# A decoder layer on one Trainium2 core: the down projection's splits and sums put in program order, twelve norm multiplications spread over six halves, and sums made ahead begun and ended sooner

## The chip, the cores and the metric

One core of a Trainium2 chip runs the whole layer in one launch. The engines named below are TensorE (PE; PEld is its weight load), VectorE (DVE), ScalarE (ACT), GpSimdE (POOL) and SyncE (SP). Each works through its own instructions in the order in which they are queued and waits on semaphores for the others; DMAs are issued from the queues of SP, ACT and POOL. The metric is device time in microseconds (us), and lower is better. The kernel before takes 1496.49 us (median of 3 runs, 1496.36 to 1498.1).

## The reference, cut to what matters

```python
BATCH, SEQ, D_MODEL, D_FF = 1, 256, 2048, 8192          # float32 throughout
def reference(x, ...):
    h = rmsnorm(x, norm_mix_pre)
    proj = h @ w_in                                      # 2048 x 13312
    xr, yr, q, k, v, g_rnn, g_attn = split(proj)
    y_rnn = rg_lru(causal_conv(xr)) * gelu(yr)
    y_att = sliding_window_sink_attention(rope(q), rope(k), v, sinks)
    mix = sigmoid(g_rnn) * (y_rnn @ w_rnn_proj) + sigmoid(g_attn) * (y_att @ w_attn_proj)
    x = x + rmsnorm(mix @ w_out, norm_mix_post)
    h = rmsnorm(x, norm_mlp_pre)
    u = square(relu(h @ w_mlp_up))                       # 256 x 8192
    x = x + rmsnorm(u @ w_mlp_down, norm_mlp_post)       # the down projection: 8192 x 2048
    return x
def rmsnorm(x, g):
    return x * rsqrt(mean(x * x, -1) + 1e-6) * g
```

## The kernel before, in words

**Tiling.** The 256 rows of x stand as two blocks of 128 (`TB = 2`). Every float32 matrix product is made of three TensorE products of two-part operands: high times high, high times low, low times high, each 128 x 128 by 128 x 512 (or 256) columns, accumulated in a PSUM bank. So each piece of weight has to be split. The class `Stream` does that for all weights in one fixed order: a weight chunk of 128 x 2048 is two halves of 128 x 1024, numbered through the whole kernel. For half j, SP loads `wraw j` (every fifth half `xraw` in the later stages), ACT copies it, rounded, to `whi j` (line 104), and DVE subtracts the two to get `wlo j` (line 105). There are 4 rooms for raw halves (`WRAW`), 6 for high parts and 6 for low parts (`WHALF`). A raw room comes free when its low part has been made, and only then SP's next load can go; a high or low room comes free when TensorE has used its content.

**The stages.** The input projections, attention, the recurrent branch and the gates take the first half of the time. Then the output projection, here the o pass (matmuls on lines 327 to 331, halves 240 to 271); then the MLP, cut into two parts f = 0 and f = 1 of 4096 columns of u each: up f = 0, down f = 0 (two column halves of the output, n = 0 from about 981 us and n = 1 from about 1063 us), up f = 1, down f = 1 (n = 0 from about 1322 us, n = 1 from about 1403 us).

**The down projection.** The 16 pairs of chunks of one (f, n) come as halves 336 to 367 (f = 0, n = 0), 368 to 399, 464 to 495 and 496 to 527. Ten of the 16 pairs (nine for f = 1) are done with seven products instead of eight (`seven`): their right operands are four quarters of the raw pair and three sums of quarters. `right_sums` (lines 59, 61 and 62) makes the three sums `t`, `t` and `t4` on DVE, `two_parts` splits the two raw halves into `whi`/`wlo`, and the inner function `split` makes `thi` (ACT, line 148) and `tlo` (DVE, line 149) of the three sums. For some of those pairs the three sums were made long before by the generator `sums_ahead` (POOL loads four quarters, DVE adds them, POOL writes the sums and the changed half away to DRAM), and come back by DMA as `second`. TensorE's products of the down projection are all on line 1178. Their banks are P1, P6, Q5, N7 (tiles `s0`, `s1`), and `dP2`, `dQ3`, `dQ4`, `dCs`.

After the last seven-product pair, `down` merges the four banks of `s0` and `s1`: an ACT copy of P1 (line 1227) and DVE sums on lines 1228 to 1231 (in f = 1 also line 1324, `early`). The last two pairs of each (f, n) are "held": their four halves stay in their rooms and are used for one output bank after the other, so that each bank is finished while TensorE works on the next. `finish` adds the merged sum to the bank: for f = 0 on line 1312, with a DMA on ACT's queue to `acc_away` behind it (line 1313); for f = 1, n = 0 on lines 1347 and 1348; for f = 1, n = 1 on lines 1352 to 1372, which end the kernel.

**What sets the order.** A scheduler places the instructions of each engine by estimated times when the kernel is built, within the dependencies. `tc.keep_in_program_order` pins an instruction behind the one traced before it on its engine; `tc.issue_after(i)` puts what a block traces behind instruction i on i's engine. In the kernel before, the splits and sums of the down projection are not pinned; a `ws.pin` that does nothing is set before the MLP.

**The norm's weight multiplications.** Before the o pass, twelve DVE multiplications of 128 x 512 are traced as a block: four of `gp` by `g2` (line 949) and eight of `x1` by `g2` (line 954).

**Sums made ahead.** `sums_ahead(c, gaps, rooms)` is run a step at a time by `ws.begin`, once per half or pair; `gaps` are the steps it waits between its loads, its sums and its writes. Six are put in the list ahead of the gates, with gaps (1, 3, 1); four are put there in up f = 0 at pair 2 (`R2_AT`), with gaps (1, 5, 1).

## Time and profile before

| | before |
|---|---|
| median of 3 runs | 1496.49 us |
| profiled execution, its own time | 1495.03 us |
| its span, first to last instruction | 1493.3 us |
| mean granted TensorE clock | 0.999 |
| PE busy | 1479.2 us (99%) |
| DVE busy | 1139.9 us (76%) |
| ACT busy | 852.7 us (57%) |
| POOL busy | 77.5 us (5%) |
| DMA, mean over the span | 229 GB/s |

The profile is one execution; the outside of its span is 1495.03 - 1493.3 = 1.7 us. A row of the timeline gives start, duration, engine, line, operation, out<-in, shapes and count, and in brackets the idle time of the engine just before with what ended it. Matmuls overlap: one 128 x 512 product starts 0.23 us after the one ahead of it though its record is 0.39 us long, so a stall of TensorE is read from starts.

### The profile page before, as it was taken

The numbers are of one execution on the slowest core, as the hardware profiler recorded it, in microseconds if no ns is written. First come the engines' busy times: TensorE is split into PE (matmuls) and PEld (weight loads), VectorE is DVE, ScalarE is ACT, GpSimd is POOL, SyncE is SP. The second block draws the span as 40 slices with busy tenths as digits, with TensorE's granted clock in tenths as the row PEclk, the third lists the DMA queues.
The fourth block names the chain that finished last, engine by engine and source line by source line (L and its number), as shares of the span: only waits on it lengthen the run. The fifth ranks groups of instructions, "written<-read, shape, count | busy, mean of one in ns | idle before, by whom it ended". The sixth has DMA issues, their size and how long they took to land.

```text
span 1493.3 us, 20560 instructions
## 1 busy us (share of the span) xinstructions
PE 1479.2 (99%) x7556; PEld 1252.9 (84%) x7556; DVE 1139.9 (76%) x1503; ACT 852.7 (57%) x1236; POOL 77.5 (5%) x149
## 2 busy tenths in 40 slices
PE   9999999999999999999999999999999999999997
PEld 7887778888888888888789888888878888888886
DVE  7676668749668866666667877799987777789897
ACT  8564565647467675444355665556564545556563
POOL 0000000000000001110000011010110111000000
PEclk9999999999999999999999999999999999999999
DMA  9754544555646667886775877678778777678584
GB/s 341 228 167 141 177 165 135 176 189 178 203 157 207 201 205 253 309 291 238 288 237 171 286 266 266 215 252 279 242 268 297 251 258 249 200 279 275 190 275 165
DMA packets 96901, 342.38 MB, mean 229 GB/s; under 512 B 11552, under 2 KB 11808, under 8 KB 95776
## 3 DMA queue, kind: packets, MB, share of 16 engines
q1 hardware_dynamic: 80352, 288.89, 57.2%
q0 software_dynamic: 12992, 44.05, 8.4%
q10 hardware_dynamic: 3456, 8.13, 1.5%
q8 instruction: 59, 0.97, 0.3%
q14 instruction: 42, 0.34, 0.1%
HBM read 316.38 MB, written 24.64 MB: 228 GB/s over the span
## 4 chain that ended last, share of the span: by engine, by line
PE 83%; DVE 9%; DMA 5%; issue 2%; ACT 1%; DVEq 0%; SPq 0%; ACTq 0%
PE ps L289 21%; PE ps L287 11%; PE g L327 4%; PE g L331 4%; PE g L329 4%; PE pp L329 4%; PE pp L327 4%; PE pp L331 4%; PE dQ L1178 4%; DVE wlo L105 3%; PE s L1178 3%; DMA wraw<-in_w_dn 3%; PE q L327 2%; PE dP L1178 2%; PE q L331 2%; PE q L329 2%
## 5 line engine op out<-in xcount | busy, mean ns | idle before, releaser
L105 DVE TENSOR_TENSOR wlo<-wraw,whi 128x1024 fp32r<-128x1024 f32 x469 | 567.7, 1221 | 240.1 <-ACT whi L104 236.3
L104 ACT CAST whi<-wraw 128x1024 fp32r<-128x1024 f32 x469 | 489.2, 1051 | 431.6 <-PE ps L289 83.1
L289 PE MATMUL ps<-h2T,whi 128*128 128x512 f32 x960 | 223.9, 390 | 0.0
L289 PEld LDWEIGHTS ps<-h2T,whi 128*128 128x128 f32 x960 | 178.2, 188 | 35.7
L287 PEld LDWEIGHTS ps<-h2T,wlo 128*128 128x128 f32 x960 | 119.1, 192 | 2.3
L289 PE MATMUL ps<-hT,whi 128*128 128x512 f32 x512 | 120.6, 391 | 0.0
L287 PE MATMUL ps<-h2T,wlo 128*128 128x256 f32 x960 | 119.9, 283 | 0.0
L289 PEld LDWEIGHTS ps<-hT,whi 128*128 128x128 f32 x512 | 94.7, 188 | 19.5 <-issue 0.7
L1178 PE MATMUL dQ<-whi,uT 128*128 128x512 f32 (+1 forms) x284 | 104.1, 385 | 0.0
L327 PE MATMUL g<-whi,hT 128*128 128x512 f32 x256 | 101.1, 395 | 0.0
L331 PE MATMUL g<-whi,hT 128*128 128x512 f32 x256 | 99.8, 390 | 0.0
L329 PE MATMUL g<-wlo,hT 128*128 128x512 f32 x256 | 99.8, 390 | 0.0
L104 ACT CAST whi<-xraw 128x1024 fp32r<-128x1024 f32 x47 | 49.4, 1051 | 33.3 <-PE ps L289 19.3
L358 POOL DMA_DIRECT2D early<-in_w_dn x56 | 30.4, 543 | 702.3 <-DVE px L317 498.0
L105 DVE TENSOR_TENSOR wlo<-xraw,whi 128x1024 fp32r<-128x1024 f32 x47 | 57.3, 1220 | 11.2 <-ACT whi L104 11.2
L287 PEld LDWEIGHTS ps<-hT,wlo 128*128 128x128 f32 x512 | 63.7, 191 | 2.1 <-issue 0.8
L287 PE MATMUL ps<-hT,wlo 128*128 128x256 f32 x512 | 64.6, 283 | 0.0
L1178 PEld LDWEIGHTS dQ<-whi,uT 128*128 128x128 f32 x284 | 53.0, 188 | 10.6
L148 ACT CAST thi<-t 128x512 fp32r<-128x512 f32 x72 | 41.3, 617 | 32.4 <-PE s L1178 14.6
L327 PEld LDWEIGHTS g<-whi,hT 128*128 128x128 f32 x256 | 48.1, 188 | 10.6 <-issue 1.0
L331 PEld LDWEIGHTS g<-whi,hT 128*128 128x128 f32 x256 | 48.0, 188 | 10.3
L329 PEld LDWEIGHTS g<-wlo,hT 128*128 128x128 f32 x256 | 48.1, 188 | 9.6
(309 smaller groups left out, 2759.3 us busy)
## 6 DMA issues: line engine op xcount, KB each, us to landing
wraw<-in_w_up SPq DMA_DIRECT2D x106, 512.0 KB, 4.8
wraw<-in_w_dn SPq DMA_DIRECT2D x93, 512.0 KB, 4.8
wraw<-in_w_g SPq DMA_DIRECT2D x64, 512.0 KB, 4.6
wraw<-in_w_xy SPq DMA_DIRECT2D x64, 512.0 KB, 4.2
wraw<-in_w_q SPq DMA_DIRECT2D x32, 512.0 KB, 3.8
wraw<-in_w_ap SPq DMA_DIRECT2D x32, 512.0 KB, 3.9
wraw<-in_w_rp SPq DMA_DIRECT2D x32, 512.0 KB, 5.0
wraw<-in_w_out SPq DMA_DIRECT2D x32, 512.0 KB, 5.0
```

The lines of the kernel that those rows point to most:

```text
L104: self.pin(self.nc.scalar.copy(hi, src))
L105: self.pin(self.nc.vector.tensor_tensor(lo, src, hi.bitcast(F32), ALU.subtract))
L148: self.nc.scalar.copy(hi, t)
L287: mm(ps[:, f, 1, :], w, a[:, 0, :], start=False, stop=j == 1 and k == 7)
L289: mm(ps[:, f].rearrange("p a b -> p (a b)"), w, a.rearrange("p a b -> p (a b)"), start=kt == 0, stop=j == 3 and k == 7)
L327: mm(banks[tb][n], a[:, 0, t], hi[:, n * 512 : n * 512 + 512], start=first, stop=False)
L329: mm(banks[tb][n], a[:, 0, t], lo[:, n * 512 : n * 512 + 512], start=False, stop=False)
L331: mm(banks[tb][n], a[:, 1, t], hi[:, n * 512 : n * 512 + 512], start=False, stop=last)
L358: nc.gpsimd.dma_start(w[:, quarter(i)], chunks[c][:, quarter(i)])
L1178: mm(b, a[x], w[y], start=not begun and i == 0, stop=tail and i == 2, skip_group_check=shared)
```

## The change

The instructions of every engine are the same in number and kind before and after; only their order changes. There are three edits.

1. **Down projection.** The three sums of a raw pair, the splits into `whi` and `wlo` (of the seven-product pairs and, through the set `plain_down`, of the others in the down stages) and the splits into `thi` and `tlo` are pinned with `tc.keep_in_program_order`.
2. **Norm's weight multiplications.** The twelve are traced inside the o pass, two behind each of the low parts 248 to 253, with `tc.issue_after`.
3. **Sums made ahead.** The gaps (1, 3, 1) become (1, 2, 1); the four of up f = 0 begin at pair 1 and have gaps (1, 4, 1) in place of (1, 5, 1); the changed half is written away ahead of the sums.

```diff
-def right_sums(v, a, b, one, two):
+def right_sums(v, a, b, one, two, pin=lambda i: i):
...
+    pin(v.tensor_tensor(b[:, l], one[:, l], a[:, r], ALU.add))
+    pin(v.tensor_tensor(two, b[:, l], b[:, r], ALU.add))
...
@@ split_to @@
+            if j // 2 in self.kept:
+                self.pin = self.keep
             self.parts[j] = self.two_parts(self.raw.pop(j), j)
+            if j // 2 in self.kept:
+                self.pin = lambda i: i
...
@@ two_parts @@
-        self.pin(self.nc.vector.tensor_tensor(lo, src, hi.bitcast(F32), ALU.subtract))
+        self.latest_low = self.pin(self.nc.vector.tensor_tensor(lo, src, hi.bitcast(F32), ALU.subtract))
...
@@ split_sums @@
-            right_sums(v, a, b, one, two)
+            right_sums(v, a, b, one, two, self.keep)
...
+        self.pin = self.keep
         (ahi, alo), (bhi, blo) = self.two_parts(a, j), self.two_parts(b, j + 1)
+        self.pin = lambda i: i
...
-                self.nc.scalar.copy(hi, t)
-                v.tensor_tensor(lo, t, hi.bitcast(F32), ALU.subtract)
+                self.keep(self.nc.scalar.copy(hi, t))
+                self.keep(v.tensor_tensor(lo, t, hi.bitcast(F32), ALU.subtract))
...
@@ sums_ahead @@
-        for away, of in ((to[:, 0:1024], one), (to[:, 1024:1536], two), (b, w[:, 1024:2048])):
+        for away, of in ((b, w[:, 1024:2048]), (to[:, 0:1024], one), (to[:, 1024:1536], two)):
...
-    pin = ws.pin = tc.keep_in_program_order
+    pin = ws.pin = ws.keep = tc.keep_in_program_order
+    ws.kept = plain_down
...
-    ws.side += [sums_ahead(c, (1, 3, 1), unit_rooms) for c in summed[:6]]
+    ws.side += [sums_ahead(c, (1, 2, 1), unit_rooms) for c in summed[:6]]
...
-    for q in range(4):
-        nc.vector.tensor_tensor(gpg2[:, quarter(q)], gp[:, quarter(q)], g2[:, quarter(q)], ALU.mult)
...
+    def times_gains(kt):
+
+        for i in range(2 * kt - 6, 2 * kt - 4) if 3 <= kt < 9 else ():
+            tb, c = i // 4 - 1, quarter(i % 4)
+            to, by = (gpg2, gp[:, c]) if i < 4 else (xg[tb], x1[:, tb, c])
+            with tc.issue_after(ws.latest_low.ins):
+                nc.vector.tensor_tensor(to[:, c], by, g2[:, c], ALU.mult)
...
-    held = o_pass(mixT, banks, HELD)
+    held = o_pass(mixT, banks, HELD, times_gains)
...
+            if f == 0 and p == 1:
+                ws.side += [sums_ahead(c, (1, 4, 1), lambda: ws.sums_rooms()) for c in summed[6:10]]
...
-                ws.side += [sums_ahead(c, (1, 5, 1), ws.sums_rooms) for c in summed[6:10]]
```

The line numbers of the changed kernel are shifted: 105 becomes 109, 148 and 149 become 154 and 155, 1178 becomes 1191, 1227 to 1231 become 1240 to 1244, 1312 becomes 1326, 1313 becomes 1327, 1324 becomes 1338, 1352 becomes 1366, 949 and 954 become 966. Three places show what moves.

**DVE in the o pass.** The names ending in a number of their own are tiles; `gpg2` and `xg0`, `xg1` are the products with the gains, `early` those of a sum made ahead. Before:

```order
L105 TENSOR_TENSOR wlo248_6352<-wraw248_6215,whi248_6351 128x1024
L949 TENSOR_TENSOR gpg2_6271<-gp_6267,g2_6269 128x512 x4
L954 TENSOR_TENSOR xg0_6276<-x1_6261,g2_6269 128x512 x4
L954 TENSOR_TENSOR xg1_6277<-x1_6261,g2_6269 128x512 x4
L105 TENSOR_TENSOR wlo249_6370<-wraw249_6299,whi249_6369 128x1024
L105 TENSOR_TENSOR wlo250_6388<-wraw250_6318,whi250_6387 128x1024
L59 TENSOR_TENSOR early_t_6405<-early_6209 128x1024
```

And in the changed kernel, on the same engine at the same place:

```order
L109 TENSOR_TENSOR wlo248_6347<-wraw248_6218,whi248_6346 128x1024
L966 TENSOR_TENSOR gpg2_6274<-gp_6270,g2_6272 128x512 x2
L109 TENSOR_TENSOR wlo249_6367<-wraw249_6294,whi249_6366 128x1024
L966 TENSOR_TENSOR gpg2_6274<-gp_6270,g2_6272 128x512 x2
L109 TENSOR_TENSOR wlo250_6387<-wraw250_6313,whi250_6386 128x1024
L966 TENSOR_TENSOR xg0_6275<-x1_6264,g2_6272 128x512 x2
L109 TENSOR_TENSOR wlo251_6407<-wraw251_6332,whi251_6406 128x1024
```

Ten of the twelve multiplications moved from ahead of `wlo249` to behind it, two by two, and the sum made ahead moved out of this stretch to an earlier place.

**DVE from down f = 0, n = 0 to n = 1.** `t_9464` and `t4_9465` are the sums of the first pair of n = 1 (halves 368 and 369), `t_9399` to `t_9402` the merged sums of n = 0. Before:

```order
L59 TENSOR_TENSOR t_9464<-wraw369_9313,wraw368_9295 128x1024
L105 TENSOR_TENSOR wlo366_9367<-wraw366_9244,whi366_9366 128x1024
L105 TENSOR_TENSOR wlo367_9371<-wraw367_9293,whi367_9370 128x1024
L61 TENSOR_TENSOR wraw369_9313<-t_9464,wraw368_9295 128x512
L105 TENSOR_TENSOR wlo368_9470<-wraw368_9295,whi368_9469 128x1024
L1228 TENSOR_TENSOR t_9400<-s0_8773,t_9399 128x512
L105 TENSOR_TENSOR wlo369_9474<-wraw369_9313,whi369_9473 128x1024
L1229 TENSOR_TENSOR t_9401<-s1_8774,t_9400 128x512
L149 TENSOR_TENSOR tlo_9478<-t_9464,thi_9477 128x512
```

In the changed kernel:

```order
L1326 TENSOR_TENSOR t_9401<-dQ3_8776,t_9401 128x512
L1326 TENSOR_TENSOR t_9399<-dP2_8775,t_9399 128x512
L1326 TENSOR_TENSOR t_9400<-dQ4_8777,t_9400 128x512
L1326 TENSOR_TENSOR t_9402<-dCs_8778,t_9402 128x512
L59 TENSOR_TENSOR t_9464<-wraw369_9313,wraw368_9295 128x1024
L61 TENSOR_TENSOR wraw369_9313<-t_9464,wraw368_9295 128x512
L62 TENSOR_TENSOR t4_9465<-wraw369_9313 128x512
L109 TENSOR_TENSOR wlo368_9470<-wraw368_9295,whi368_9469 128x1024
L109 TENSOR_TENSOR wlo369_9474<-wraw369_9313,whi369_9473 128x1024
L155 TENSOR_TENSOR tlo_9478<-t_9464,thi_9477 128x512
```

The sums and splits of halves 368 and 369 stood ahead of the merge and of the four finishing sums of n = 0, and now stand behind all of these, the last of which reads `dCs`.

**ACT at the same place.** `acc_away` are the DMAs that carry the four finished tiles off. Before:

```order
L104 CAST whi368_9469<-wraw368_9295 128x1024
L1227 COPY t_9399<-s0_8773 128x512
L104 CAST whi369_9473<-wraw369_9313 128x1024
L148 CAST thi_9477<-t_9464 128x512
L148 CAST thi_9481<-t_9464 128x512
L1313 DMA acc_away_6264<-t_9401 128x512
L1313 DMA acc_away_6264<-t_9399 128x512
L148 CAST thi_9485<-t4_9465 128x512
```

In the changed kernel:

```order
L1240 COPY t_9399<-s0_8773 128x512
L1327 DMA acc_away_6267<-t_9401 128x512
L1327 DMA acc_away_6267<-t_9399 128x512
L1327 DMA acc_away_6267<-t_9400 128x512
L1327 DMA acc_away_6267<-t_9402 128x512
L108 CAST whi368_9469<-wraw368_9295 128x1024
L108 CAST whi369_9473<-wraw369_9313 128x1024
L154 CAST thi_9477<-t_9464 128x512
L154 CAST thi_9481<-t_9464 128x512
L154 CAST thi_9485<-t4_9465 128x512
```

The high parts of the first pair and of its sums moved behind the four DMAs. TensorE's own order around here is the same in both kernels up to the first product of n = 1, `s1<-thi_9477`, which follows the last `dCs` product directly.

**DVE at the end of down f = 1, n = 1.** `t_13232` to `t_13235` are the merged sums, 526 and 527 the last two halves of all. Before:

```order
L105 TENSOR_TENSOR wlo526_13246<-wraw526_13133,whi526_13245 128x1024
L1228 TENSOR_TENSOR t_13233<-s0_12655,t_13232 128x512
L105 TENSOR_TENSOR wlo527_13250<-wraw527_13176,whi527_13249 128x1024
L1229 TENSOR_TENSOR t_13234<-s1_12656,t_13233 128x512
L1324 TENSOR_TENSOR t_13232<-t_13232,acc1_11919 128x512
L1230 TENSOR_TENSOR t_13233<-t_13233,s1_12656 128x512
L1231 TENSOR_TENSOR t_13235<-t_13234,s1_12656 128x512
L1324 TENSOR_TENSOR t_13233<-t_13233,acc0_11918 128x512
L1324 TENSOR_TENSOR t_13234<-t_13234,acc1_11919 128x512
L1324 TENSOR_TENSOR t_13235<-t_13235,acc0_11918 128x512
L1352 TENSOR_TENSOR acc0_11918<-dQ4_12659,t_13233 128x512
```

In the changed kernel:

```order
L1241 TENSOR_TENSOR t_13233<-s0_12655,t_13232 128x512
L1242 TENSOR_TENSOR t_13234<-s1_12656,t_13233 128x512
L1338 TENSOR_TENSOR t_13232<-t_13232,acc1_11919 128x512
L1243 TENSOR_TENSOR t_13233<-t_13233,s1_12656 128x512
L1244 TENSOR_TENSOR t_13235<-t_13234,s1_12656 128x512
L1338 TENSOR_TENSOR t_13233<-t_13233,acc0_11918 128x512
L1338 TENSOR_TENSOR t_13234<-t_13234,acc1_11919 128x512
L1338 TENSOR_TENSOR t_13235<-t_13235,acc0_11918 128x512
L109 TENSOR_TENSOR wlo526_13246<-wraw526_13133,whi526_13245 128x1024
L109 TENSOR_TENSOR wlo527_13250<-wraw527_13176,whi527_13249 128x1024
L1366 TENSOR_TENSOR acc0_11918<-dQ4_12659,t_13233 128x512
```

The two low parts moved behind the eight merging sums. TensorE follows: its last three products into `dQ4`, which use `wlo526` and `wlo527`, stood directly behind those of half 525 and now stand behind the `dCs` products of halves 524 and 525 and six `dP2` products, the product with `wlo527` as the 38th from the first with half 522, where it was the 23rd.

17 lines of the change are left out of this document (7 added, 10 removed).

## The prediction

> **What bounds the kernel now.** I read the page's busy time first, then the list of what TensorE waits for, then TensorE's timeline around each of those waits, then DVE's and ACT's timelines there, and last the windows at the kernel's end.
>
> ```profile
> PE 1479.2 (99%) x7556; PEld 1252.9 (84%) x7556; DVE 1139.9 (76%) x1503; ACT 852.7 (57%) x1236; POOL 77.5 (5%) x149
> ...
> PE s L1178 <- DVE tlo L149: 1.6, 1, 1.6
> PE s L1178 <- DVE u L317: 1.2, 1, 1.2
> ...
> PE o L329 <- DVE wlo L105: 0.8, 1, 0.8
> PE dQ L1178 <- DVE tlo L149: 0.3, 1, 0.3
> ...
> PE o L327 <- ACT whi L104: 0.2, 1, 0.2
> ```
>
> TensorE is the bound, and no product is added or removed. So the change can gain only what TensorE waits in the middle of the kernel, 4.1 us by these five rows, and can lose wherever a new wait arises. The true stalls are read from starts:
>
> ```profile
> 744.14 0.39 PE L331 MATMUL o<-whi,mixT 128*128 128x512 f32 x1
> 744.69 0.49 PE L327 MATMUL o<-whi,mixT 128*128 128x512 f32 x1 [0.17 <-ACT whi L104]
> 745.95 0.50 PE L329 MATMUL o<-wlo,mixT 128*128 128x512 f32 x1 [0.77 <-DVE wlo L105]
> ...
> 983.05 0.39 PE L1178 MATMUL dQ<-wlo,uT 128*128 128x512 f32 x1
> 984.64 0.50 PE L1178 MATMUL s<-whi,three 128*128 128x512 f32 x1 [1.20 <-DVE u L317]
> 984.98 0.39 PE L1178 MATMUL s<-wlo,three 128*128 128x512 f32 x1
> ...
> 1062.30 0.39 PE L1178 MATMUL dCs<-whi,uT 128*128 128x512 f32 x1
> 1062.52 0.39 PE L1178 MATMUL s<-thi,uT 128*128 128x512 f32 x1
> ...
> 1114.88 0.39 PE L1178 MATMUL s<-thi,uT 128*128 128x512 f32 x1
> 1116.86 0.50 PE L1178 MATMUL s<-tlo,uT 128*128 128x512 f32 x1 [1.58 <-DVE tlo L149]
> ...
> 1404.74 0.39 PE L1178 MATMUL dQ<-thi,three 128*128 128x512 f32 x1
> 1405.41 0.50 PE L1178 MATMUL dQ<-tlo,three 128*128 128x512 f32 x1 [0.29 <-DVE tlo L149]
> ```
>
> Undisturbed starts are 0.23 us apart (1062.30 to 1062.52), and the step behind a stall is 0.34 (984.64 to 984.98), so each stall costs 0.11 more. That makes 0.32 + 1.03 + 0.11 = 1.46 in the o pass; 1.36 + 0.11 = 1.47 at the start of down f = 0; 1.75 + 0.11 = 1.86 at 1116.86; 0.44 + 0.11 = 0.55 at 1405.41. The ceiling of the gain is 5.34 us.
>
> **Part by part. The multiplications.**
>
> ```profile
> 725.78 2.50 DVE L949 TENSOR_TENSOR gpg<-gp,g 128x512 f32<-128x512 f32 x4 [5.42 <-DMA gp<-in_gains]
> ...
> 733.01 2.35 DVE L105 TENSOR_TENSOR wlo<-wraw,whi 128x1024 fp32r<-128x1024 f32 x2
> ...
> 743.59 1.05 ACT L104 CAST whi<-wraw 128x1024 fp32r<-128x1024 f32 x1 [1.82 <-DMA wraw<-in_w_out]
> ```
>
> The block holds back `wlo249` until 733.01, so raw rooms come free late, the next loads are issued late, and the `whi` of 743.59 waits 1.82 us for its DMA: this is the o pass stall. Behind `wlo248` the first pair of multiplications still waits for `gp` (725.78). Then low parts of 1.14 us (half of 2.35 back to back) alternate with pairs of 1.2 us: `wlo249` ends near 729.4 instead of 734.2, `wlo251`, whose room the last late load needs, some 3.5 us sooner than before. The stall of 1.46 goes with about 2 us to spare. No instruction is added; moving the early sum ahead of these halves costs nothing, since DVE stood idle 5.42 us there.
>
> **Sums made ahead.** Four of them end sooner in up f = 0.
>
> ```profile
> 979.57 1.23 DVE L59 TENSOR_TENSOR t<-wraw,wraw 128x1024 f32<-128x1024 f32 x1 [1.58 <-DMA away<-t]
> ...
> 1322.66 0.59 ACT L316 COPY u<-ps 128x512 f32<-128x512 f32 x1 [3.82 <-PE ps L289]
> ...
> 1323.28 0.69 DVE L317 TENSOR_TENSOR u<-ps,u 128x512 f32<-128x512 f32 x1 [2.58 <-ACT u L316]
> ```
>
> DVE's wait of 1.58 us for the last sum's write delays the drain of the up product's bank (984.64 above). Without it, ACT's copy and DVE's sum should run as in f = 1, where nothing stands ahead of them and no wait of TensorE follows: the bank is free 1.31 us after the copy's start (1322.66 to 1323.97). In f = 0 the copy can start near 981.0 (the first of ten products ahead of 983.05 starts at 980.78), so the bank is free at 982.3, and TensorE, which by the new order goes on with `s0` at 982.82, has 0.5 us to spare. I book 1.47. Waits that the earlier sums put before DVE in the gates and the up stage lie on an engine idle 24% of the time; I take nothing, bounds 0 and 1.5 (the wait above).
>
> **The pins: two stalls less.**
>
> ```profile
> 1111.38 1.23 DVE L59 TENSOR_TENSOR t<-wraw,wraw 128x1024 f32<-128x1024 f32 x1 [3.37 <-DMA wraw<-in_w_dn]
> ```
>
> This sum waited 3.37 us for a raw half with two low parts and the needed `tlo` behind it. Now these stand ahead: `tlo` near 1111 instead of 1116.8. The 1.86 go. At 1405.41 the pinned order also makes `tlo` about 3 us sooner: 0.55.
>
> **The pins: one stall more.** From n = 0 to n = 1 of f = 0, the orders shown put the sum `t_9464`, its splits and everything behind them after the finishing sum that reads `dCs`, and `dCs` is finished by the very last product before TensorE needs `thi_9477` (1062.30 and 1062.52 above). The chain's prices:
>
> ```profile
> 1141.70 0.39 PE L1178 MATMUL dQ<-whi,uT 128*128 128x512 f32 x1
> ...
> 1142.12 0.69 DVE L1312 TENSOR_TENSOR t<-dQ,t 128x512 f32<-128x512 f32 x1 [1.79 <-PE dQ L1178]
> ...
> 1057.44 1.22 DVE L59 TENSOR_TENSOR t<-wraw,xraw 128x1024 f32<-128x1024 f32 x1
> 1058.57 0.68 DVE L1312 TENSOR_TENSOR t<-dP,t 128x512 f32<-128x512 f32 x1
> 1059.17 0.68 DVE L61 TENSOR_TENSOR wraw<-t,xraw 128x512 f32<-128x512 f32 x1
> ...
> 1064.77 0.33 ACTq L1313 DMA_DIRECT2D acc_away<-t  x1
> 1065.21 1.05 ACT L104 CAST whi<-wraw 128x1024 fp32r<-128x1024 f32 x1 [1.17 <-DVE t L1312]
> 1066.16 1.66 ACT L148 CAST thi<-t 128x512 fp32r<-128x512 f32 x3
> ```
>
> From a bank's last product to its sum 0.42 (1141.70 to 1142.12): 1062.72. Then DVE's pace: finishing sum 0.60 (1058.57 to 1059.17), L59 1.13 (1057.44 to 1058.57): L61 starts at 1064.45 and ends at 1065.14. ACT passes the DMA in 0.44 and `whi368` is done by 1064.9; `whi369` needs L61, starts at 1065.17, and 0.95 later (1065.21 to 1066.16) comes `thi_9477`, 1066.12 to 1066.74. TensorE starts at 1066.8 instead of 1062.52: 4.28 us. More follows, because DVE and ACT start n = 1 with nothing in hand: the third `thi` (0.52 apart) is ready at 1067.85, needed at 1067.38 (0.47); `tlo_9478` behind L62 and two low parts at 1068.68, needed at 1068.42 (0.26); `wlo370`, behind the `tlo` and three more sums, at 1073.36, needed at 1072.87 (0.49). With four restarts of 0.11: 4.28 + 1.22 + 0.44 = 5.94 us. Bounds: 4.3 if nothing follows, 7 if each later item of that pair is late by half a microsecond too.
>
> **The pins: the end.**
>
> ```profile
> 1468.80 0.39 PE L1178 MATMUL dQ<-whi,uT 128*128 128x512 f32 x1
> ...
> 1469.00 0.59 ACT L1227 COPY t<-s 128x512 f32<-128x512 f32 x1 [0.26 <-PE s L1178]
> ...
> 1475.91 0.68 DVE L1352 TENSOR_TENSOR acc<-dQ,t 128x512 f32<-128x512 f32 x1
> ...
> 1485.55 0.42 DVE L1352 TENSOR_TENSOR acc<-s,t 128x256 f32<-128x256 f32 x1 [1.08 <-PE s L1178]
> ```
>
> `wlo526` and `wlo527` now follow the copy (1469.6) and eight sums of 0.60: 1475.6 and 1476.8. TensorE's new order wants them no sooner than 1476.0 and 1477.2, so it does not wait; but `dQ4` is finished at its 39th product from 1468.80, started at 1477.41, and its finishing sum runs at 1477.83 instead of 1475.91. That is 1.92 later at the head of a DVE chain that had 1.08 us of idle time ahead of its last part: the kernel ends 0.84 later. Bounds 0 and 1.92.
>
> **Sum.** Low parts and `tlo` from 1404 to 1428 and from 1068 to 1084 have margins of 0.1 to 0.3 us by the same reckoning; I add 0.3 for those that miss. 1495.03 (the profiled execution) - 5.34 + 5.94 + 0.84 + 0.30 = 1496.77. The median of the runs is 1.46 above that execution, so 1498.2 us, 0.1% over the median before. About 0.2%, 3 us, can be told from no change.
>
> **Rivals.** *TensorE's clock falls in the new gap.*
>
> ```profile
> 1485.50:1486.50 1.00, 0.01 (x1) 0.00 (x0) 0.85 (x2) 0.49 (x2) 0.00 (x0) 1.00 0.00 0
> ...
> 1488.50:1489.50 1.00, 0.00 (x0) 0.00 (x0) 1.00 (x3) 0.00 (x0) 0.00 (x0) 0.90 0.64 236
> 1489.50:1490.50 1.00, 0.00 (x0) 0.00 (x0) 0.51 (x1) 0.00 (x0) 0.00 (x0) 0.50 1.02 375
> ```
>
> Behind the last product (1485.5) the granted clock stays 1.00, is 0.90 in the window of 1488.5 and 0.50 from there: it fell at 1489.3, after 3.8 us of idleness. The new gap is idle for some 4.1 us, just beyond. If the clock stays at half as long as it took to fall, 1.9 us are lost: 1500.1, slower. It decides when the gap outlasts 3.8 us in this phase; against it, the later waits of 1.2 us absorb part. [...]
>
> *DVE is too full from 1404 to 1428.* There the first plain splits now stand behind the finishing sums and two multiplications by `g3` (1.2 us). TensorE's order has other products put in between; if these don't cover, TensorE waits some 1.7 us (1.2, and 1.13 for an L59 that ran ahead of the `dCs` sum before, less 0.6 that DVE catches up): 1499.9, slower.
>
> *The change doesn't do what it says:* with the start of down f = 0 kept late (its margin is 0.5) and another 1 us kept elsewhere, 1498.2 + 2.5 = 1500.7.
>
> *The new wait is not paid,* if the sums of n = 1 ran before the `dCs` sum after all: 1498.2 - 5.9 = 1492.3, faster. The orders shown speak against it.
>
> **Chances.** My sum 0.52; the clock 0.17; DVE too full 0.14; stalls kept 0.09; not paid 0.08. The likeliest gives 1498.2, with 1496.0 to 1499.5 its own range. From 1495.0 (0.84 and most of what follows the 4.28 not paid) to 1502.0 (two of the slower cases) about 0.15 is left out. Faster by over 0.2%: 0.08; within: 0.52; slower: 0.40.
>
> **What would show it.** In the profile after, the waits at 744, 984, 1116 and 1405 should be missing; TensorE should wait about 4.2 us on `thi` from ACT near 1059.6 (1062.5 less the first two stalls), with smaller waits on `thi`, `tlo` and `wlo` behind it; the first `dQ` finishing sum of the end should come about 2 us later after the last `s` copy than before; the clock should read 1.00 behind the gap. The prediction is wrong if that gap is absent, longer than 7 us, or followed by a clock of 0.50, or if new waits stand in the gates or the up stages.

## The result, and the profile after

The changed kernel takes 1503.69 us (median of 6 runs, 1502.68 to 1506.92). The kernel before, run again beside it, takes 1496.40 us (median of 6 runs, 1494.33 to 1498.1). The ratio is 1.0053, with a 95% interval of 1.0040 to 1.0066: slower by half a per cent. The profiled execution takes 1503.92 us, with a span of 1502.2 us and a mean granted clock of 0.995; before it was 0.999. The ratios of the experiments are against runs of the kernel before from their own round (medians 1495.2 to 1495.9 us); the quotient of two medians can differ from such a ratio by 0.001. Two runs at a much lower granted clock are left out: one of the kernel before (2256.32 us at 0.613) and one of experiment 5 (1637.13 us at 0.848).

TensorE's waits in the profile after, in the same columns as before (us in total, times, longest):

```profile
PE s L1191 <- ACT thi L154: 4.3, 1, 4.3
PE ptr L901 <- DVE g L919: 3.6, 1, 3.6
...
PE s L1191 <- DVE tlo L155: 0.5, 1, 0.5
```

The waits of before on `wlo` and `whi` in the o pass, on `u`, and on `tlo` at 1116.86 and 1405.41 are gone. The 4.3 us on `thi` were foreseen, in size a little short (see below). The 3.6 us on `g` were not: they stand in the gates, for which the prediction had booked nothing.

To see what each place costs, I took the start of the same product of TensorE in both traces, place by place. The measured column is the step of that difference at the place:

| place (time before) | measured, us | in the prediction's sum, us |
|---|---|---|
| gates (604 to 612) | +5.37 | 0 (bounds 0 and 1.5) |
| o pass (744 to 746) | -1.50 | -1.46 |
| start of down f = 0 (984) | -1.12 | -1.47 |
| f = 0, n = 0 to n = 1 (1062 to 1079) | +6.89 | +5.94 |
| `tlo`, at 1085 | +0.76 | in the 5.94 |
| 1116.86 | -1.88 | -1.86 |
| 1405.41 | -0.56 | -0.55 |
| behind 1405 | +0.34 | +0.30 |
| end | +0.63 | +0.84 |
| sum, span against span | +8.9 | +1.74 |

The gates and the way from n = 0 to n = 1 (with the `tlo` behind it) miss; the other six places came out within 0.4 us of the sum. For "behind 1405" this is luck: the sum had its 0.30 for late parts from 1404 to 1428 and from 1068 to 1084, and most of the 0.34 arises near 1434. Of the 7.2 us that the sum lacked, 5.4 are the gates and 1.7 the place between n = 0 and n = 1.

**The gates.** VectorE's timeline before:

```profile
587.78 1.23 DVE L105 TENSOR_TENSOR wlo<-wraw,whi 128x1024 fp32r<-128x1024 f32 x1 [1.20 <-ACT whi L104]
...
599.18 1.23 DVE L105 TENSOR_TENSOR wlo<-wraw,whi 128x1024 fp32r<-128x1024 f32 x1 [0.56 <-ACT whi L104]
600.32 1.28 DVE L910 SCALAR_TENSOR_TENSOR g<-g,pp 128x512 f32<-128x512 f32 x2
```

VectorE's timeline after, at the same work:

```profile
588.09 1.23 DVE L59 TENSOR_TENSOR early_t<-early 128x1024 f32<-128x1024 f32 x1 [2.88 <-DMA early<-in_w_dn]
589.23 1.22 DVE L109 TENSOR_TENSOR wlo<-wraw,whi 128x1024 fp32r<-128x1024 f32 x1
...
591.70 3.49 DVE L109 TENSOR_TENSOR wlo<-wraw,whi 128x1024 fp32r<-128x1024 f32 x3
...
603.00 1.23 DVE L109 TENSOR_TENSOR wlo<-wraw,whi 128x1024 fp32r<-128x1024 f32 x1 [4.04 <-ACT whi L108]
604.14 1.28 DVE L918 SCALAR_TENSOR_TENSOR g<-g,pp 128x512 f32<-128x512 f32 x2
605.34 1.28 DVE L919 TENSOR_TENSOR g<-g,m 128x512 f32<-128x512 f32 x2
```

The second of the six sums made ahead (L59, 588.09) now stands between `wlo198` and `wlo199` (the row of 589.23), and waits 2.88 us there for its own load. The row of 587.78 before is `wlo200`; after, it is the first of the three low parts from 591.70, 3.9 us later. When `wlo200` is done, its raw room is free and SP issues the load of `raw204`: at 589.03 before, at 592.94 after. The chain of work that ended last holds that load:

```profile
592.94 8.88 DMA wraw<-in_w_g
```

It lands 8.88 us later, so `wlo204` is made at 603.00 and not at 599.18. TensorE has no use for `wlo204` yet. But the gates' product stands behind it in VectorE's queue, and TensorE's transposes wait for that product. TensorE's timeline after:

```profile
602.08 0.39 PE L338 MATMUL g<-whi,hT 128*128 128x512 f32 x1
606.08 0.66 PE L901 MATMUL ptr<-ident,g 128*128 128x128 f32 x4 [3.61 <-DVE g L919]
```

Before, these transposes start at 602.36: 3.72 us sooner. The rest of the 5.37 is the clock.

**The clock.** Windows after, with the span of time, the busy times and instructions of PE, PEld, DVE, ACT and POOL, and then the granted clock, the DMA share and GB/s:

```profile
602.00:606.00 4.00, 0.47 (x3) 0.04 (x1) 3.00 (x5) 2.01 (x2) 0.00 (x0) 1.00 1.03 406
606.00:607.00 1.00, 0.92 (x6) 0.84 (x7) 1.00 (x3) 0.00 (x0) 0.00 (x0) 0.86 1.03 402
607.00:610.00 3.00, 3.00 (x9) 2.35 (x8) 1.98 (x2) 1.93 (x2) 0.00 (x0) 0.50 0.79 284
610.00:611.00 1.00, 1.00 (x6) 0.83 (x5) 0.81 (x1) 0.66 (x2) 0.00 (x0) 0.93 0.94 299
...
1067.00:1068.00 1.00, 0.00 (x0) 0.00 (x0) 0.95 (x2) 0.57 (x1) 0.00 (x0) 0.76 0.68 254
1068.00:1074.00 6.00, 4.32 (x10) 2.88 (x11) 5.95 (x8) 3.55 (x5) 0.00 (x0) 0.50 0.46 135
1074.00:1075.00 1.00, 1.00 (x5) 0.82 (x4) 0.97 (x2) 0.28 (x1) 0.00 (x0) 0.82 0.55 225
```

The clock reads 1.00 ahead of the row of 606.00 and 0.50 behind it, so 0.86 there means 0.50 for 0.28 us of the row: the clock fell at 606.72. By the same reckoning it came back at 610.14, fell again at 1067.52 and came back at 1074.36. At 0.50 TensorE's products of 128 x 512 start 0.43 us apart (607.27 to 607.70), at 1.00 0.23. In the gates TensorE works through 3.42 us at 0.50, called half speed below, which costs 1.7 us by the clock's share (1.62 by experiment 4). Before, the clock reads 1.00 up to 1489 and falls only behind the last product.

**From n = 0 to n = 1.** TensorE after:

```profile
1065.01 0.39 PE L1191 MATMUL dCs<-whi,uT 128*128 128x512 f32 x1
1069.68 0.80 PE L1191 MATMUL s<-thi,uT 128*128 128x512 f32 x1 [4.28 <-ACT thi L154]
```

The row's idle time is 4.28 us. Counted from starts, as the prediction counts a stall, it is 4.45 (1069.68 - 1065.01 = 4.67, less the 0.22 of an undisturbed step), where the sum had 4.28. Behind it TensorE works at half speed from 1069.68 to 1074.36, which loses 2.3 us more. But it is not the clock that sets what the stretch costs. VectorE after, from the sum that reads `dCs` on, and then TensorE's next wait:

```profile
1065.43 0.69 DVE L1326 TENSOR_TENSOR t<-dCs,t 128x512 f32<-128x512 f32 x1 [2.03 <-PE dCs L1191]
...
1088.30 3.49 DVE L109 TENSOR_TENSOR wlo<-wraw,whi 128x1024 fp32r<-128x1024 f32 x3
1093.56 1.22 DVE L109 TENSOR_TENSOR wlo<-wraw,whi 128x1024 fp32r<-128x1024 f32 x1 [1.77 <-ACT whi L108]
1094.70 1.89 DVE L155 TENSOR_TENSOR tlo<-second,thi 128x512 fp32r<-128x512 f32 x3
```

```profile
1095.43 0.50 PE L1191 MATMUL s<-tlo,uT 128*128 128x512 f32 x1 [0.48 <-DVE tlo L155]
```

The chain of work that ended last goes through these rows of VectorE and this load, and not through TensorE:

```profile
1085.47 6.93 DMA wraw<-in_w_dn
```

From 1065.43 VectorE has no pause until 1091.79. Then it waits for the half of this load, which goes out only when a low part of the same stretch has ended (at 1085.44), and the `tlo` that comes of it lets TensorE go on at 1095.43. This wait ends last, so up to here the loss is 7.65 us (6.89 and 0.76), set by VectorE and that load. What TensorE loses to the clock on the way only makes its wait for this `tlo` shorter: experiment 5 has the comparison that shows it.

**The end.** The first finishing sum of the last bank group stood 6.91 us behind the copy of `s` before (1469.00 to 1475.91). VectorE after:

```profile
1482.79 2.35 DVE L109 TENSOR_TENSOR wlo<-wraw,whi 128x1024 fp32r<-128x1024 f32 x2
1486.07 0.69 DVE L1366 TENSOR_TENSOR acc<-dQ,t 128x512 f32<-128x512 f32 x1 [0.93 <-PE dQ L1191]
...
1494.56 0.42 DVE L1366 TENSOR_TENSOR acc<-s,t 128x256 f32<-128x256 f32 x1
```

The copy starts at 1477.23 now, so the sum comes 8.84 us behind it, 1.93 later than before. The last sum (1494.56) has lost the 1.08 us of idle time that stood ahead of it.

### The profile page after: what moved, and what is told of

Its sections match the earlier page's. It is cut to its first block, busy times and chain, and to the rows that moved or that the text cites. A ratio compares the mean times of both kernels' runs of the same rounds, so it can differ in the third digit from the quotient of the medians.

```text
span 1502.2 us, 20543 instructions
## 1 busy us (share of the span) xinstructions
PE 1483.7 (99%) x7556; PEld 1255.6 (84%) x7556; DVE 1143.2 (76%) x1503; ACT 852.3 (57%) x1236; POOL 77.6 (5%) x149
## 4 chain that ended last, share of the span: by engine, by line
PE 91%; DVE 4%; DMA 2%; ACT 2%; issue 1%; DVEq 0%; ACTq 0%
PE ps L296 21%; PE ps L294 11%; PE dQ L1191 7%; PE s L1191 6%; PE dP L1191 4%; PE pp L338 3%; PE pp L334 3%; PE pp L336 3%; PE g L334 3%; PE g L338 3%; PE g L336 3%; PE dCs L1191 2%; PE q L334 2%; PE q L338 2%; PE q L336 2%; PE o L336 2%
## 5 line engine op out<-in xcount | busy, mean ns | idle before, releaser
L1191 PE MATMUL s<-thi,uT 128*128 128x512 f32 x152 | 54.1, 397 | 4.3 <-ACT thi L154 4.3
```

The lines of the kernel that those rows point to most:

```text
L1191: mm(b, a[x], w[y], start=not begun and i == 0, stop=tail and i == 2, skip_group_check=shared)
```

## The experiments

The changed kernel has three edits, and two places lose time. The theory: the wait in the gates comes from one number, the gap (1, 2, 1), which puts one sum into VectorE's queue at a bad place; the wait between n = 0 and n = 1 comes from the pins alone; and the clock falls because TensorE stands idle. The rivals are in the expectations. An execution of one kernel differs from the next by 1 to 2 us as a rule, but the runs of one kernel can lie 9 us apart (experiment 6); so the ratios carry intervals, and the places are read from the traces, each of which is one execution.

This table gives, for each kernel, how far the same product of TensorE stands behind the kernel before (us, at the times of before; from the profiled executions):

| kernel | 619 | 754 | 1002 | 1079 | 1102 | 1131 | 1418 | end |
|---|---|---|---|---|---|---|---|---|
| changed | 5.32 | 3.82 | 2.71 | 9.60 | 10.36 | 8.48 | 7.84 | 8.89 |
| 1 old gate gaps | -0.23 | -1.73 | -2.83 | 3.76 | 4.83 | 2.95 | 2.31 | 3.42 |
| 2 gate gap alone | 2.41 | 2.10 | 1.86 | 1.86 | 2.20 | 2.76 | 3.33 | 3.27 |
| 3 second sum later | 0.18 | 0.95 | 3.71 | 3.71 | 3.71 | 3.52 | 2.69 | 2.63 |
| 4 products in the wait | 3.29 | 1.78 | 1.71 | 8.24 | 9.32 | 7.45 | 6.80 | 7.61 |
| 5 pins alone | -0.20 | -0.68 | -1.90 | 5.03 | 5.92 | 4.04 | 3.40 | 4.44 |
| 6 no pins | 3.09 | 1.58 | 0.08 | 0.08 | 0.89 | 3.36 | 2.81 | 2.73 |
| 7 up sums alone | -0.08 | -0.78 | -2.29 | -1.23 | -0.62 | 2.39 | 2.18 | 2.12 |
| 8 gains alone | -0.14 | -1.64 | -0.46 | -0.46 | -0.46 | -1.57 | -1.83 | -1.94 |
| 9 first pair free | -0.26 | -1.77 | -2.89 | -0.51 | -0.33 | -2.21 | -2.85 | -1.45 |
| 10 first and last free | 0.02 | -1.49 | -2.62 | -1.33 | -1.33 | -3.21 | -3.83 | -3.61 |

### 1. The gates' old gaps in the changed kernel

```diff
-    ws.side += [sums_ahead(c, (1, 2, 1), unit_rooms) for c in summed[:6]]
+    ws.side += [sums_ahead(c, (1, 3, 1), unit_rooms) for c in summed[:6]]
```

> The changed kernel with one number put back: the steps of the sums made ahead in the gates spread by (1, 3, 1) again instead of (1, 2, 1). The new order of the three writes stays. Theory A (with the shorter gap the second sum made ahead falls between two low parts of one pair, holds wlo199 and wlo200 back by 3.9 us, and through their raw rooms the load of raw204, behind whose low part the gates' product stands on VectorE): the wait of TensorE's transposes for g near 604 (3.6 us) and the fall of its clock behind it are gone, TensorE stands within 0.5 us of the kernel before at 608 instead of 5.3 behind, and the time is 1503.7 - 5.3 = 1498.4 us, ratio 1.001. Rival B (the order of the writes does it, the copy of b now being the first): the wait stays and the time is 1503 to 1504. The waits later in the kernel, 4.3 us on thi between the halves of the down projection f = 0 above all, stay under both.

Measured: 1499.16 us, ratio to before 1.0031 (1.0019 to 1.0043); 1498.4 was expected. TensorE's longest waits, and VectorE in the gates:

```profile
PE s L1191 <- ACT thi L154: 4.3, 1, 4.3
...
PE s L1191 <- DVE tlo L155: 0.8, 1, 0.8
```

```profile
598.58 1.22 DVE L109 TENSOR_TENSOR wlo<-wraw,whi 128x1024 fp32r<-128x1024 f32 x1 [0.55 <-ACT whi L108]
599.72 1.28 DVE L918 SCALAR_TENSOR_TENSOR g<-g,pp 128x512 f32<-128x512 f32 x2
```

The wait on `g` is gone, and with it what the clock's fall behind it cost: TensorE stands at -0.23 us at 619. The new order of the writes, which stayed, does no harm here. The wait between n = 0 and n = 1 is untouched. Theory A holds.

### 2. The gates' gap alone in the kernel before

```diff
-    ws.side += [sums_ahead(c, (1, 3, 1), unit_rooms) for c in summed[:6]]
+    ws.side += [sums_ahead(c, (1, 2, 1), unit_rooms) for c in summed[:6]]
```

> The kernel before with one number changed: the gaps of the six sums made ahead in the gates are (1, 2, 1) instead of (1, 3, 1). Theory A (this number alone makes the wait in the gates): TensorE waits 2.7 to 3.6 us on g near 604, and with the restart, and the fall of the clock if it comes (it came in the changed kernel, and not in the one without pins), stands 3.1 to 5.3 us behind the kernel before at 612; the rest as before, so 3 to 5 us slower, near 1499.5 us, ratio 1.003. Rival B (the new order of the three writes is needed too): no wait there, ratio 1.000.

Measured: 1499.9 us, ratio 1.0030 (1.0019 to 1.0041).

```profile
PE ptr L893 <- DVE g L911: 2.5, 1, 2.5
```

The number alone is enough to make the wait. It is 2.5 us here and not 3.6, and the clock did not fall (1.00 from 602 to 610), so TensorE stands 2.4 us behind at 619: less than the 3.1 to 5.3 expected. In the profiled execution another 0.9 was lost by the end, and it takes 1498.3 us; the median of the 12 runs, 1.6 us above it, came out as expected (1499.5). Whether the clock falls in the slower of these runs is not shown.

### 3. The second sum behind the gates' product

```diff
-    ws.side += [sums_ahead(c, (1, 3, 1), unit_rooms) for c in summed[:6]]
+    ws.side += [sums_ahead(c, (1, 4 if i == 1 else 2, 1), unit_rooms) for i, c in enumerate(summed[:6])]
```

> The kernel just described, with the gaps of the second of the six sums alone made longer, (1, 4, 1), so that its three additions stand behind the gates' product on VectorE as in the kernel before, and not between wlo198 and wlo200; the first sum, and the third to the sixth, keep (1, 2, 1). Theory A (the place of this one sum on VectorE is the cause): no wait on g over 0.3 us, and the time of the kernel before, ratio 1.000. Rival B (sums that are loaded sooner crowd the DMA engines, so that raw204 lands late wherever the sum stands): the wait stays, with a ratio near 1.003.

Measured: 1497.33 us, ratio 1.0002 (0.9992 to 1.0013). VectorE in the gates:

```profile
596.40 1.22 DVE L105 TENSOR_TENSOR wlo<-wraw,whi 128x1024 fp32r<-128x1024 f32 x1 [0.55 <-ACT whi L104]
597.54 1.28 DVE L910 SCALAR_TENSOR_TENSOR g<-g,pp 128x512 f32<-128x512 f32 x2
...
602.28 1.22 DVE L59 TENSOR_TENSOR early_t<-early 128x1024 f32<-128x1024 f32 x1
```

No wait on `g` is left. The first sum still has the short gap, so it is the place of the second sum that makes the wait. This does not exclude that the later loads of the third to sixth sums, which moved with it, help a little. (The profiled execution is 2.6 us longer than before mostly for another reason, a wait at 984 with a fall of the clock; see the last section.)

### 4. Products in the gates' wait

```diff
             ps = bank(psg, "ptr")
+            if n == 0 and tb == 0:
+                full = flat(yrnn[0])[:, 0:512]
+                for i in range(14):
+                    pin(mm(ps, full[:, 0:P], full, start=True, stop=True))
```

> The changed kernel with 14 products of 128 x 128 by 128 x 512 more, whose result is overwritten and used nowhere; TensorE does them in the gates' wait, just ahead of the transposes that wait for g. The wait itself stays. At 0.23 us each they take 3.2 of the 3.6 us. Theory A (the granted clock falls because TensorE stands idle there): the clock stays 1.00 behind the transposes, TensorE stands 3.6 to 4.0 us behind the kernel before at 612 instead of 5.3, and the time is 1.5 us below the changed kernel's, near 1502.2 us. Rival B (the clock falls for another cause, the stage's heavy DMA say): it falls behind the transposes all the same and the time is that of the changed kernel, 1503 to 1504.

Measured: 1502.48 us, ratio 1.0039 (1.0027 to 1.0052). TensorE, and the windows behind the transposes:

```profile
602.50 3.34 PE L903 MATMUL ptr<-yrnn 128*128 128x512 f32 x14
605.67 0.60 PE L905 MATMUL ptr<-ident,g 128*128 128x128 f32 x4
```

```profile
606.00:607.00 1.00, 1.00 (x7) 0.86 (x6) 1.00 (x1) 0.90 (x1) 0.00 (x0) 1.00 0.99 389
607.00:610.00 3.00, 3.00 (x14) 2.44 (x14) 1.78 (x3) 1.76 (x4) 0.00 (x0) 1.00 0.83 272
```

With the same heavy DMA (0.99 of its time, where it was 1.03), the clock stays at 1.00. TensorE stands 3.29 us behind at 619 and not 5.32 (3.6 to 4.0 was expected). Of the 2.03 between them, 0.41 is that the transposes could start sooner in this execution (605.67, not 606.08); 1.62 is the clock. Without the products the wait would be 3.17 us long here (602.50 to 605.67), between the 2.89 us at which the clock stayed at 1.00 in experiment 6 and the 3.33 us at which it fell in experiment 7 (last section). So theory A fits, with idle time making the clock fall and useless products keeping it up, but that it would have fallen in this execution without them is not shown. Against rival B, the heavy DMA alone did not make it fall.

### 5. The pins alone in the kernel before

```diff
-    pin = ws.pin = tc.keep_in_program_order
+    pin = ws.pin = ws.keep = tc.keep_in_program_order
+    ws.kept = plain_down
```

(and the calls of edit 1 that use them)

> The kernel before with edit 1 alone: the down projection's splits and sums in program order; gates, up stage and multiplications as before. Theory A (the pinned order is the whole cause of the wait between n = 0 and n = 1 of f = 0): TensorE waits about 4.3 us on thi near 1065, its clock falls behind it, 6.9 us are lost there and 0.8 more on tlo near 1090, the waits at 1117 (1.9) and 1405 (0.6) go, and the end takes 0.7 longer: 5.9 us slower than the kernel before, near 1501.5 us, ratio 1.004. Rival B (the earlier sums of edit 3 are needed for it): no wait over 2 us there and a ratio of 1.000 or less.

Measured: 1500.3 us, ratio 1.0025 (1.0016 to 1.0034).

```profile
PE s L1186 <- ACT thi L154: 4.3, 1, 4.3
```

The wait on `thi` is the same 4.3 us, with 6.89 us lost there: the pins alone make it. The ratio is below the 1.004 expected since the wait at 984 went as well, which I had put down to edit 3. The pins put `wlo338` behind the sums ahead of it; the `u` sum that drains the up product's bank then ends at 982.3 and not at 984.6. So the two edits both remove that wait, each by itself.

Four profiled kernels have this wait, and they show what the clock's fall costs behind it. The second column is how much of TensorE's work lay in the time at half speed, the last is from the start of the sum that reads `dCs` on VectorE to the start of TensorE's product with the `tlo` shown above:

| kernel | worked at half speed, us | wait for the `tlo`, us | from the `dCs` sum to that product, us |
|---|---|---|---|
| changed | 4.67 | 0.48 | 30.00 |
| 1 old gate gaps | 3.41 | 0.79 | 30.01 |
| 4 products in the wait | 3.41 | 0.78 | 29.96 |
| 5 pins alone | 4.67 | 0.61 | 30.12 |

In the changed kernel TensorE works 1.26 us longer at half speed than in experiment 1 and loses 0.63 us more of work by the clock's share, but the product comes at the same time to 0.01 us; the wait for the `tlo` is shorter by 0.31 us of it, and the rest of the difference lies in delays of 0.1 us and less ahead of that. So VectorE's queue sets the 30 us, and the clock's fall is hidden in them. No kernel here has the wait without any fall; that this would not be sooner either is inferred.

### 6. The changed kernel without the pins

```diff
-    pin = ws.pin = ws.keep = tc.keep_in_program_order
-    ws.kept = plain_down
+    pin = ws.pin = tc.keep_in_program_order
+    ws.keep = lambda i: i
```

> The changed kernel without edit 1 (down projection's splits and sums issued when the scheduler takes them, as before); gates and multiplications as changed. Theory A (the pinned order alone makes the wait on thi between n = 0 and n = 1 of f = 0, the fall of the clock there and the longer tail): TensorE loses 6.9 + 0.8 + 0.6 us less behind 988 us of the span, and pays again the 1.9 and 0.6 us that the kernel before waits at 1117 and 1405, so the time is 1503.7 - 5.8 = 1497.9 us, ratio 1.001; the 3.6 us wait in the gates stays. Rival B (the earlier sums in up f = 0 have moved the down projection's loads, and its waits come from there): 1502 to 1504, with a wait on thi of 3 us or more near 1066.

Measured: 1500.12 us, ratio 1.0029 (1.0016 to 1.0042). The wait between n = 0 and n = 1 and the longer end are gone, as theory A says, but the median is 2 us above it. The profiled execution itself takes 1497.77 us, which is theory A's time, with two larger misses in opposite directions. The gates cost 3.1 us and not 5.3, since the wait on `g` is 2.7 us there and not 3.6 and the clock did not fall there in this execution (1.00 from 602 to 610). And at 1117 TensorE loses 2.4 us more than the kernel before does, with a fall of the clock (its mean over this execution is 0.997), where I had expected just the old 1.9 again, and 0.8 more near 1101. Neither theory had this; the next kernel shows it by itself. The 12 runs spread from 1493.35 to 1502.35 us, and which of the two misses the slower ones have is not shown.

### 7. The up stage's sums alone in the kernel before

```diff
+            if f == 0 and p == 1:
+                ws.side += [sums_ahead(c, (1, 4, 1), lambda: ws.sums_rooms()) for c in summed[6:10]]
...
-                ws.side += [sums_ahead(c, (1, 5, 1), ws.sums_rooms) for c in summed[6:10]]
```

> The kernel before with the up stage's part of edit 3 alone: the four sums made ahead in up f = 0 begun at pair 1 and spread by (1, 4, 1), with the old order of the writes. Theory A (the last sum stands behind its write's landing on VectorE, which holds back the drain of the up product's bank): the wait of 1.2 us at 984.6 is gone, and nothing else moves: 1495.0 us, ratio 0.999. Rival B (the old order of the writes matters here: the last write is that of the copy of b, and VectorE's last sum still waits for it): 1496.2 to 1497, the wait stays.

Measured: 1496.12 us, ratio 1.0004 (0.9994 to 1.0015). The wait at 984 is gone: TensorE gains 1.5 us there. In the profiled execution, the slowest of the 12 runs, it keeps none of it, and the median shows no gain either. SP's queue before, and then in this kernel:

```profile
1068.16 5.06 SPq L86 DMA_DIRECT2D wraw<-in_w_dn  x2
```

```profile
1068.19 5.06 SPq L86 DMA_DIRECT2D wraw<-in_w_dn  x2
```

TensorE comes up to 2.3 us sooner behind 984, and the loads go up to 6.2 us sooner there (one at 1005.70 that went at 1011.94). But by 1032 the loads have lost this lead (1032.35 for 1032.26), and from 1064 to 1107 they go within 0.22 us of their old times, except one that goes 1.27 later. So here TensorE's time does not set the loads'. That the ring of raw rooms, of load, split and next load, sets them is inferred, and where the lead goes between 1005 and 1032 is not shown. TensorE then waits longer for the same `tlo`:

```profile
1114.33 0.39 PE L1186 MATMUL s<-thi,uT 128*128 128x512 f32 x1
1117.88 0.79 PE L1186 MATMUL s<-tlo,uT 128*128 128x512 f32 x1 [3.17 <-DVE tlo L155]
```

It waits 3.17 us where it was 1.58. About 1.0 of the difference is a load that landed later in this execution (VectorE's sum behind it starts at 1112.40, not at 1111.38); the rest is TensorE's lead. The clock falls near the end of this wait (half speed from 1117.36 to 1120.78, of which TensorE works the last 2.9), which costs 1.4 more by the clock's share. The gain of edit 3 was real at 984 and was gone at 1117 in this execution.

### 8. The multiplications alone in the kernel before

```diff
+    def times_gains(kt):
...
-    held = o_pass(mixT, banks, HELD)
+    held = o_pass(mixT, banks, HELD, times_gains)
```

> The kernel before with edit 2 alone: the twelve multiplications by the norm's weights spread over six halves of the o pass. Theory A (the block of multiplications holds wlo249 back, and with it the raw rooms): the waits at 744.7 and 745.9 are gone, and nothing else moves: 1.5 us sooner, 1494.9 us, ratio 0.999. Rival B (in the changed kernel the 1.5 us were gained only since TensorE came 5.3 us later there, and the loads had that much more time): the waits stay, wholly or in part, and the time is 1495.5 to 1496.5.

Measured: 1494.81 us, ratio 1.0000 (0.9991 to 1.0009). The waits in the o pass are gone and TensorE gains 1.50 there, as theory A has it. But the waits that follow take from it: 0.64 near 824 on VectorE's `st`, and 0.54 more at 984, where the wait on `u` grows to 1.7. The profiled execution ends 1.94 us sooner since it lost less at 1117; the median of 12 runs doesn't show a gain.

### 9. One pair left out of the pinned order

The old gate gaps, and the pair of halves 368 and 369, the first of f = 0, n = 1, not pinned.

```diff
-    ws.kept = plain_down
+    ws.kept, ws.free = plain_down, {184}
...
+            keep = (lambda i: i) if j // 2 in self.free else self.keep
-            right_sums(v, a, b, one, two, self.keep)
+            right_sums(v, a, b, one, two, keep)
```

(and the same for its splits)

> The changed kernel with the gates' old gaps (1, 3, 1), and with one pair of edit 1 left out of the pinned order: halves 368 and 369, the first of f = 0, n = 1, with its sums and splits. On VectorE the sum of 368 and 369 then stands ahead of the four finishing sums of n = 0 again, as in the kernel before; everything behind it is pinned. Theory A (this one pair behind the four finishing sums makes the wait): the wait on thi of 4.3 us near 1064 and the fall of the clock are gone, and the kernel keeps what the change gains: o pass 1.7, start of down f = 0 1.3, at 1117 1.9, at 1405 0.6, less 0.7 at the end: 4.8 us faster than the kernel before, near 1490.5 us, ratio 0.997. Rival B (the ring of raw rooms does not run sooner, whatever TensorE does, so that what is gained ahead of 990 us is waited for by 1117): 1 to 2 us faster than before, near 1494, ratio 0.999.

Measured: 1493.88 us, ratio 0.9985 (0.9975 to 0.9995).

```profile
PE s L1192 <- DVE tlo L156: 1.2, 2, 1.0
...
PE s L1192 <- DVE wlo L109: 0.5, 1, 0.5
```

No wait on `thi`, and no fall of the clock before the end (1.00 up to 1487). That one pair, behind the four finishing sums, made the wait. Of TensorE's lead of 2.89 us, 2.4 goes on the way from n = 0 to n = 1: VectorE is not that far ahead, and `wlo` and `tlo` come late by 0.5 to 1.0 us. The 1.9 at 1117 is gained all the same, which rival B had not allowed. Still the time is rival B's (near 1494) and 3.4 us above theory A's: the wait that theory A is about is gone, but its forecast that everything gained is kept is wrong.

### 10. The last pair left out too

```diff
-    ws.kept, ws.free = plain_down, {184}
+    ws.kept, ws.free = plain_down, {184, 263}
```

> The kernel just described with one more pair left out of the pinned order: halves 526 and 527, the last of the kernel, whose low parts stand behind four sums of the merge on VectorE when pinned. Theory A (they cost the 0.6 to 0.9 us at the end): the end is as in the kernel before, and the time 0.7 us below the other's, which the traces show and the times hardly. Rival B (the end is longer for another reason): no difference between the two.

Measured: 1492.57 us, ratio 0.9971 (0.9958 to 0.9983). From 1482 to the end the kernel with only the first pair free loses 0.80 us against before; this one gains 0.11. The longer end is the pinned place of `wlo526` and `wlo527`. In its profile TensorE waits once in the middle of the kernel:

```profile
PE s L1192 <- DVE tlo L156: 1.0, 1, 1.0
```

This is the fastest of all kernels here, 0.3% faster than the one before. It has neither of the change's two new waits. Of the change's gains it loses 1.3 us on the way from n = 0 to n = 1, where the kernel of experiment 9 lost 2.4 in its execution.

## Why the prediction was wrong

The forecast was 1498.2 us, with 1495.0 to 1502.0 as the range; it is 1503.69.

**The step that failed** is the sentence on the sums made ahead: "Waits that the earlier sums put before DVE in the gates and the up stage lie on an engine idle 24% of the time; I take nothing, bounds 0 and 1.5". It cost 5.37 us. A mean idle share over the kernel says nothing on who stands behind the waiting instruction. There stood `wlo199` and `wlo200`, behind these a raw room, a load of 8.9 us and `wlo204`, and behind that the gates' product. The halves had slack enough (TensorE did not wait for one of them), but VectorE took its queue in order (`wlo204` at 603.00, then `g` at 604.14) and handed their delay to a product that had none. The upper bound of 1.5 came from a wait in another stage, where no ring of rooms stands behind. The prediction itself named new waits in the gates among the things that would make it wrong. The order on VectorE is fixed when the kernel is built, so the place could be seen beforehand; the prediction followed that order at the places where TensorE waited before, and not wherever it had changed.

**A second term, too small,** is what follows the wait between n = 0 and n = 1: 1.22 us for late parts and 0.44 for restarts, 1.66 in all. It measured 3.20 (7.65 less the 4.45 of the wait). The prediction had the cause right, that VectorE and ACT start n = 1 with nothing in hand, but it followed VectorE only as far as `wlo370`, ready at 1073.36 by its reckoning. VectorE stays full for 26 us, and the `tlo` that ends the stretch stands behind a load that goes out only 20 us into that stretch, at 1085.47. The bound of 7 us for the whole place was passed with it.

**The clock's fall** was a rival with a chance of 0.17 and a price of 1.9 us. It fell in all four profiled kernels that have the 4.3 us wait on `thi` (the changed kernel, 1, 4 and 5). The condition was wrong: "when the gap outlasts 3.8 us", read from one fall behind the last product. The clock also fell at waits of 3.77, 3.33, 2.56 and 2.17 us (below), and what decides at the shorter ones is not shown. Its price was wrong for this place too: half speed loses 2.3 us of TensorE's work there by the clock's share, but the `tlo` comes no sooner without that, so the loss is hidden (experiment 5). Where the fall did cost time, 1.6 us, was in the gates (experiment 4), where no rival had put it.

**Right by mechanism and size:** the o pass (1.50 for 1.46), 1116.86 (1.88 for 1.86), 1405.41 (0.56 for 0.55), the wait itself between n = 0 and n = 1 (4.45 for 4.28, both from starts; that the profile's idle time is 4.28 as well is chance, since it is counted from the modelled end of the last product), the first `dQ` sum at the end (1.93 for "about 2") and the end (0.63 for 0.84; experiment 10 shows its cause).

**Right in size, not alone in cause:** the start of down f = 0 (1.12 for 1.47). Edit 3 removes that wait by itself (experiment 7), but so do the pins (experiment 5).

**Not seen:** that gains ahead of 1060 can be lost again as long as the wait at 1116.86 stays. The sum booked each gain by itself. In the changed kernel this did no harm since the pins take that wait away; in the profiled executions of experiments 6 and 7 it ate the gain, in that of experiment 8 it did not.

**The other rivals:** VectorE too full from 1404 to 1428 did not come (0.1 us or less there in the changed kernel). No stall was kept, and the new wait was paid.

## What to carry to other kernels

When work is moved in an in-order queue, follow what stands behind each instruction that can now wait, through rooms and loads to the next product, at every place where the order changed; an engine's mean idle share gives no bound (24% here, and 5.37 us lost). A gain ahead of a stretch whose loads do not run on that engine's time can become a longer wait in that stretch (3.17 us for 1.58 in experiment 7). And a wait of TensorE can have a second price (here the clock fell at eight waits of 2.17 to 4.44 us): check the granted clock behind it before costing it by its length, and then whether a later wait, set by another engine, hides that price.

## What the hardware showed that I had not expected

The clock fell at waits much shorter than 3.8 us, and not at every wait of the same length. In the changed kernel it fell at 606.72 and at 1067.52 and stayed at half for 3.42 and 6.84 us. This table has, for waits in the profiled executions, how long TensorE stood idle (from 0.23 us behind the start of the last product to the start of the next), and what the granted clock did in that time or just behind it:

| kernel and wait | idle, us | clock |
|---|---|---|
| 1, n = 0 to 1 | 4.44 | fell, 3.41 us of work at half |
| 4, n = 0 to 1 | 4.44 | fell, 3.42 us at half |
| changed, n = 0 to 1 | 4.44 | fell, 6.84 us at half |
| 5, n = 0 to 1 | 4.44 | fell, 6.82 us at half |
| changed, gates | 3.77 | fell, 3.42 us at half |
| 7, at 1117 | 3.33 | fell, 3.42 us at half |
| 6, gates | 2.89 | stayed |
| 2, gates | 2.65 | stayed |
| 6, at 1118 | 2.56 | fell |
| 3, at 984 | 2.17 | fell, 3.42 us at half |
| 2, at 1118 | 2.17 | stayed |
| 8, at 984 | 1.89 | stayed |
| before, at 1117 | 1.74 | stayed |

So the length of the wait alone does not decide: the clock fell at 2.17 us in experiment 3, and not at the same 2.17 us in experiment 2, nor at 2.89 us in experiment 6. TensorE in experiment 3 and then in experiment 6:

```profile
984.37 0.39 PE L1178 MATMUL dQ<-wlo,uT 128*128 128x512 f32 x1
986.77 0.79 PE L1178 MATMUL s<-whi,three 128*128 128x512 f32 x1 [2.01 <-DVE u L317]
```

```profile
602.28 0.39 PE L338 MATMUL g<-whi,hT 128*128 128x512 f32 x1
605.41 0.44 PE L901 MATMUL ptr<-ident,g 128*128 128x128 f32 x2 [2.74 <-DVE g L919]
```

The rows with the granted clock behind them, experiment 3 and then experiment 6:

```profile
986.00:987.00 1.00, 0.23 (x1) 0.23 (x2) 1.00 (x3) 1.00 (x2) 0.00 (x0) 0.88 0.54 127
987.00:990.00 3.00, 3.00 (x8) 2.32 (x9) 3.00 (x4) 3.00 (x6) 0.00 (x0) 0.50 0.87 307
```

```profile
607.00:610.00 3.00, 3.00 (x14) 2.46 (x14) 1.74 (x3) 1.73 (x4) 0.00 (x0) 1.00 0.79 265
```

In the table the clock fell at each of the six waits of 3.33 us or more and stayed at the two of 1.89 us or less; of the five from 2.17 to 2.89 us it fell at two. What decides there is not shown. A fall of 3.42 us in which TensorE works throughout loses 1.7 us of its work by the clock's share; this is time lost in the gates (1.62, experiment 4), and not where a later wait hides it (experiment 5).
